# A fourth wide product in 14 of 22 feed-forward blocks, and a few reordered steps around the feed-forward part

## The chip, the cores and the metric

The kernel runs on one core of one Trainium2 chip. The metric is device time in microseconds of one execution; the time quoted for a kernel is the median of its runs. TensorE is called PE, VectorE DVE, ScalarE ACT, GpSimd POOL and SyncE SP, as in the profile.

## What is computed

One layer of a decoder on 512 tokens of width 1024 in float32: a mixer sublayer (stick-breaking attention beside a gated short convolution), cross-attention into 256 memory tokens, a SwiGLU feed-forward sublayer, a final norm. The change touches the feed-forward sublayer and the norm:

```python
def rms_norm(x, g):
    xf = x.astype(jnp.float32)
    var = jnp.mean(xf * xf, axis=-1, keepdims=True)
    return (xf * lax.rsqrt(var + EPS) * g.astype(jnp.float32)).astype(x.dtype)
...
        hf = rms_norm(x, norm_ffn[l])
        gate, up = jnp.split(hf @ w_ffn_in[l], 2, axis=-1)
        x = x + (jax.nn.silu(gate) * up) @ w_ffn_out[l]
    return rms_norm(x, norm_final)
```

The hidden width is 2816, which is 22 blocks of 128 gate columns and 128 up columns.

## The kernel before

**Two halves of a number.** PE multiplies in a shortened float32 format (F32R). Each operand is split: `hi` is its cast to F32R (on ACT), `lo` the rest (a subtraction on DVE: `rest_of`, L996). A product is then three multiplications: hi x hi, hi x lo, lo x hi.

**Seven products for eight.** The feed-forward input projection uses a scheme of the Strassen kind. The activations are cut in two along the tokens (256 each) and in two along the inner dimension; the weights likewise, and gate and up take the place of two output halves. `forms_of` makes seven activation forms (xf, xo, xc, a form of xd, xc, xd, xo, counted 0 to 6), and each weight block m has seven weight forms. So a block m is seven products (m, 0) to (m, 6), each over four inner slices k. They accumulate in three PSUM banks: z for the products 0, 3, 4, 5, v for 1, y for 2 and 6. `banks[m]` also holds the scratch tiles s ("sa"), t ("sb") and g ("fg").

**Narrow and wide products.** In `product` the products 0, 3, 4 and 5 are narrow: per slice three multiplications of 256 columns into the left half of z. The products 1, 2 and 6 are wide: their form lies with hi and lo side by side in one tile, so that one multiplication of 512 columns does hi x hi into the left half of the bank and hi x lo into the right (L906), and one of 256 columns adds lo x hi (L914). The halves of the bank are added when it is read (`joined_halves`, L932 and L933).

**Reading the results.** After the products 0, 3 and 4 ACT copies z to s or t (`reads`, L940). DVE joins v and y with those copies into g and t. `evict(m, 0..2)` then scales g by the norm's factor (L954), takes its silu on ACT (L956), and multiplies it by z and by t on DVE (L964): these are the activations for the output projection. `evict(m, 2)` runs one block later, at the product (m + 2, 0).

**Weights.** `ffn_load` brings a block's weights in with SP's DMA queue and adds two quarters with an accumulating DMA on POOL's queue. `sum_third` (L871) and `sum_last` (L875) make two more sums, on POOL for the blocks 0 to 2 and on DVE from 3 on. `pair_cast` and `third_cast` make the forms: a cast on ACT, and one or two products later the subtraction on DVE.

**Order.** The list `uses` gives the order of the products on PE: for a block m, (m,3), (m,2), (m,4), (m+1,0), (m+1,1), (m,5), (m,6). `todo` says which other step is issued after which entry of it (`at`, and `made` for a cast and its subtraction). PE, ACT and DVE execute in exactly that written order; each engine waits at an instruction whose operands are not there, and everything behind it waits too. PSUM gives four banks to z, two to v and two to y; the weight forms have four buffers each for hi and lo.

**The norm ahead of the feed-forward part.** The residual stream's squares are summed while the products already run, and `squares_mean` splits the sum in hi and lo (acch, accl). Two multiplications with a constant matrix give the mean (varb), then `rstd_of` makes the factor r0b: Ln and Exp on ACT, and a Newton step on DVE. Before the change these are issued after the entries 8 and 10 of `uses`.

**The end of the feed-forward part.** The casts and subtractions for the output projection's first blocks are interleaved with the last products (`begun`, `ended`; "w0" is a weight block, "x0" an activation).

## Time and profile before

| | us |
|---|---|
| median of 3 runs (lowest to highest) | 841.49 (841.46 to 842.75) |
| the profiled execution, its own time | 841.48 |
| its span in the trace | 839.8 |
| PE busy | 830.6 |
| DVE busy | 682.0 |
| ACT busy | 458.3 |
| POOL busy | 164.2 |
| feed-forward input products on PE, first to last | 502.6 to 723.8 |

A timeline row reads: start in us from the span's start, duration in us, engine, line, operation, what it writes from what it reads, shapes, count. A bracket at its end gives the time that the engine stood idle just before it and what ended this. Matmuls overlap: PE's pace is the distance of starts, and an end is modelled. In the feed-forward part the tile names say which product a row is: z<-xf is product 0, v<-xo 1, y<-xc 2, z<-xdh and z<-xdl 3 or 5, z<-xc 4, y<-xo 6.

### The profile page before, as it was taken

Reading aid. Unit: us, or ns where it says so; the run is one execution under the profiler, and the core shown is the slowest. Engines: PE = TensorE matmul, PEld = TensorE weight load, DVE = VectorE, ACT = ScalarE, POOL = GpSimd, SP = SyncE. Lnnn points to the kernel's source line nnn. Section 1 sums busy time; section 2 is a strip of 40 time slices with the busy share of each in tenths; the row PEclk is TensorE's granted clock in tenths of the full one; section 3 lists DMA queues with packets and bytes.
Section 4 is the critical chain, followed back from the end, with each engine's and each line's share of the span. In section 5 each row is a group of like instructions: output and inputs, shape, how many; then the busy total and the mean of one; then the engine's idle time right before and its main releaser. Section 6 shows DMA issues by size and latency. Waiting matters only on the chain.

```text
span 839.8 us, 12035 instructions
## 1 busy us (share of the span) xinstructions
PE 830.6 (99%) x4430; PEld 716.8 (85%) x4430; DVE 682.0 (81%) x1070; ACT 458.3 (55%) x778; POOL 164.2 (20%) x170
## 2 busy tenths in 40 slices
PE   9999999999999999999999999999999999999996
PEld 7888888888888888888888889999999999888885
DVE  7879899986756577586555689999999999999886
ACT  7567878674332355433444556644455545576654
POOL 0011131110666620173000032111111110000401
PEclk9999999999999999999999999999999999999999
DMA  8553454134687865556421326577767663465552
GB/s 302 153 167 101 121 115 112 61 121 167 235 314 274 314 230 199 188 229 235 151 75 51 101 65 161 152 180 198 200 170 204 179 181 96 165 216 197 178 184 101
DMA packets 51359, 143.70 MB, mean 171 GB/s; under 512 B 5762, under 2 KB 7042, under 8 KB 48483
## 3 DMA queue, kind: packets, MB, share of 16 engines
q1 hardware_dynamic: 41650, 107.89, 38.1%
q0 software_dynamic: 9360, 34.75, 15.6%
q8 instruction: 35, 0.57, 0.3%
q10 hardware_dynamic: 288, 0.28, 0.1%
q14 instruction: 26, 0.20, 0.1%
HBM read 125.20 MB, written 13.64 MB: 165 GB/s over the span
## 4 chain that ended last, share of the span: by engine, by line
PE 97%; DVE 1%; ACT 0%; issue 0%; DVEq 0%
PE z L911 14%; PE p L1216 12%; PE pr L156 8%; PE pr L158 8%; PE pr L157 8%; PE y L906 5%; PE r L157 3%; PE r L156 3%; PE r L158 3%; PE v L284 3%; PE v L906 2%; PE y L914 2%; PE km L662 2%; PE mq L158 2%; PE mq L156 2%; PE mq L157 2%
## 5 line engine op out<-in xcount | busy, mean ns | idle before, releaser
L151 ACT CAST wh<-wr 128x1024 fp32r<-128x1024 f32 x84 | 88.1, 1051 | 142.2 <-issue 75.3
L152 DVE TENSOR_TENSOR wl<-wr,wh 128x1024 fp32r<-128x1024 f32 x84 | 111.1, 1323 | 31.7 <-ACT wh L151 31.7
L156 PE MATMUL pr<-xgh,wh 128*128 128x512 f32 x288 | 112.8, 392 | 0.0
L157 PE MATMUL pr<-xgl,wh 128*128 128x512 f32 x288 | 112.3, 390 | 0.0
L158 PE MATMUL pr<-xgh,wl 128*128 128x512 f32 x288 | 112.2, 390 | 0.0
L607 POOL TENSOR_TENSOR pre<-pre 128x512 f32<-128x512 f32 x44 | 71.2, 1623 | 31.4 <-DMA pre<-in_w_ffn_out_dram 29.1
L859 POOL DMA_DIRECT2D ws<-in_w_ffn_in_dram x22 | 26.6, 1209 | 236.3 <-DVE c L704 53.9
L911 PE MATMUL z<-xdh,wf 128*128 128x256 f32 x352 | 70.0, 283 | 0.0
L158 PEld LDWEIGHTS pr<-xgh,wl 128*128 128x128 f32 x288 | 54.1, 188 | 11.6
L156 PEld LDWEIGHTS pr<-xgh,wh 128*128 128x128 f32 x288 | 54.1, 188 | 10.5
L157 PEld LDWEIGHTS pr<-xgl,wh 128*128 128x128 f32 x288 | 54.1, 188 | 10.5
L940 ACT COPY sa<-z 128x256 f32<-128x256 f32 x44 | 16.4, 373 | 78.9 <-PE z L911 76.7
L911 PEld LDWEIGHTS z<-xdh,wf 128*128 128x128 f32 x352 | 57.4, 190 | 0.1
L911 PE MATMUL z<-xdl,wf 128*128 128x256 f32 x176 | 49.7, 282 | 0.0
L996 DVE TENSOR_TENSOR wf<-wg,wf 128x1024 fp32r<-128x1024 f32 (+1 forms) x44 | 43.1, 979 | 1.6 <-ACT wf L884 0.2
L996 DVE TENSOR_TENSOR wl<-wr,wh 128x1024 fp32r<-128x1024 f32 x33 | 41.0, 1243 | 2.8 <-ACT wh L1063 2.8
L1063 ACT CAST wh<-wr 128x1024 fp32r<-128x1024 f32 x33 | 34.5, 1049 | 6.2 <-ACT f01h L992 2.6
L911 PE MATMUL z<-xf,wf 128*128 128x256 f32 x264 | 35.7, 283 | 0.0
L911 PE MATMUL z<-xc,wf 128*128 128x256 f32 x264 | 35.2, 283 | 0.2 <-ACT sa L940 0.2
L911 PEld LDWEIGHTS z<-xf,wf 128*128 128x128 f32 x264 | 33.4, 192 | 0.3 <-DVE wf L996 0.2
L911 PEld LDWEIGHTS z<-xc,wf 128*128 128x128 f32 x264 | 33.1, 190 | 0.5 <-ACT sa L940 0.4
L911 PEld LDWEIGHTS z<-xdl,wf 128*128 128x128 f32 x176 | 33.4, 190 | 0.0
(352 smaller groups left out, 2212.0 us busy)
## 6 DMA issues: line engine op xcount, KB each, us to landing
wr<-in_w_in_dram SPq DMA_DIRECT2D x36, 512.0 KB, 3.5
pre<-in_w_ffn_out_dram POOLq DMA_DIRECT2D x11, 1024.0 KB, 7.9
sums<-pre POOLq DMA_DIRECT2D x11, 1024.0 KB, 4.8
ws<-in_w_ffn_in_dram SPq DMA_DIRECT2D x22, 512.0 KB, 5.3
wg<-in_w_ffn_in_dram SPq DMA_DIRECT2D x22, 512.0 KB, 4.7
ws<-in_w_ffn_in_dram POOLq DMA_DIRECT2D x22, 512.0 KB, 5.8
wr<-sums SPq DMA_DIRECT2D x22, 512.0 KB, 3.9
wr<-in_w_ffn_out_dram SPq DMA_DIRECT2D x16, 512.0 KB, 4.0
```

Source lines behind the costliest of these rows:

```text
L151: after(nc.scalar.copy(h2, raw), lead[-1:])
L152: lows.append(nc.vector.tensor_tensor(out=l2, in0=raw, in1=f(h2), op=ALU.subtract))
L156: nc.tensor.matmul(ps, a[0], b[0], start=start, stop=False, **kw)
L157: nc.tensor.matmul(ps, a[0], b[1], start=False, stop=False, **kw)
L158: nc.tensor.matmul(ps, a[1], b[0], start=False, stop=stop, **kw)
L607: nc.gpsimd.tensor_tensor(out=t[:, a, :], in0=t[:, a, :], in1=t[:, b, :], op=ALU.add)
L859: nc.gpsimd.dma_start(s13, a[:, 0:4:3, :], accum_op=ALU.add)
L906: nc.tensor.matmul(ps, hi, both[0], start=i < 3 and k == 0, stop=False, skip_group_check=True)
L911: nc.tensor.matmul(ps[:, :HS], a, b, start=i < 3 and k == 0 and j == 0, stop=k == KP - 1 and j == 2, skip_group_check=True)
L996: nc.vector.tensor_tensor(out=lo, in0=src, in1=f(hi), op=ALU.subtract)
L1063: nc.scalar.copy(hi, raw)
L1216: nc.tensor.matmul(res[i][s2], a[:, ts], b, start=j == 0 and n == 0, stop=n == 2 and j == (BEHIND - 1 if (i, s2) == (5, 1) else NJ - 1))
```

## The change

1. **The sixth product is wide in 14 blocks.** `forms_of` lays the forms 3 and 5 with hi and lo side by side, as it did the others: two casts and two subtractions of 256 columns in place of one each of 512. In the blocks 5 to 18 (`WIDE`) product 5 takes the wide branch, into the whole of z. ACT then copies z's right half to s, and `evict(m, 2)` adds it to z's left half on DVE before the multiplication. The order of the products stays.
2. **The norm's factor.** `rstd_of` folds two DVE operations into one. The sum's split is issued after entry 6 in place of 8, the mean after 8 in place of 10, its DVE part after 9.
3. **Two sums change their engine.** `sum_third(2)` and `sum_last(2)` run on DVE in place of POOL. One cast is issued an entry earlier.
4. **The last two blocks.** `sum_last(21)` is issued after (20,4) in place of (21,1); the cast of its result one entry earlier; the cast "x0" one entry later.

DVE around the mean, before (acch and accl are the split sum; ra and r0b the factor; wf the weight forms):

```order
L996 TENSOR_TENSOR wf_4867<-ws_4757,wf_4866 128x1024
L932 TENSOR_TENSOR sb_4786<-y_4804,sb_4786 128x256
L933 TENSOR_TENSOR sb_4786<-y_4804,sb_4786 128x256
L996 TENSOR_TENSOR wf_4915<-wg_4840,wf_4914 128x1024
L196 CAST acch_4929<-acc_4354 128x512
L197 TENSOR_TENSOR accl_4930<-acc_4354,acch_4929 128x512
L932 TENSOR_TENSOR fg_4797<-y_4804,sa_4785 128x256
L933 TENSOR_TENSOR fg_4797<-y_4804,fg_4797 128x256
L996 TENSOR_TENSOR wf_4946<-a_4761,wf_4945 128x1024
L126 TENSOR_SCALAR rv_4963<-varb_4960 128x512
L128 TENSOR_TENSOR ra_4965<-ry_4964 128x512
L129 SCALAR_TENSOR_TENSOR ra_4965<-ra_4965,rv_4963 128x512
```

and now:

```order
L1006 TENSOR_TENSOR wf_4869<-ws_4759,wf_4868 128x1024
L201 CAST acch_4906<-acc_4348 128x512
L202 TENSOR_TENSOR accl_4907<-acc_4348,acch_4906 128x512
L1006 TENSOR_TENSOR wf_4904<-wg_4842,wf_4903 128x1024
L936 TENSOR_TENSOR sb_4788<-y_4806,sb_4788 128x256
L937 TENSOR_TENSOR sb_4788<-y_4806,sb_4788 128x256
L129 SCALAR_TENSOR_TENSOR ra_4939<-ry_4938 128x512
L131 SCALAR_TENSOR_TENSOR ra_4939<-varb_4935,ra_4939 128x512
L133 SCALAR_TENSOR_TENSOR r0b_4940<-ra_4939,ry_4938 128x512
L936 TENSOR_TENSOR fg_4799<-y_4806,sa_4787 128x256
L937 TENSOR_TENSOR fg_4799<-y_4806,fg_4799 128x256
L1006 TENSOR_TENSOR wf_4956<-a_4763,wf_4955 128x1024
```

The split sum moved ahead of a subtraction and of the pair that reads y; the factor is made ahead of the next pair, with three operations in place of four; the sum wg (L874) follows the last row shown.

ACT at the end of the feed-forward part (the copies of z, the last block's casts, "w0" as wh, "x0" as f01h), before:

```order
L940 COPY sa_7209<-z_7208 128x256
L884 CAST wf_7226<-ws_7015 128x1024
L884 CAST wf_7255<-a_7095 128x1024
L1063 CAST wh_7260<-wr_7258 128x1024
L992 CAST f01h_7263<-a_5063 128x512
L940 COPY sa_7209<-z_7208 128x256
L1000 CAST fh_7282<-a_5064 128x256
```

and now:

```order
L946 COPY sa_7182<-z_7181 128x256
L887 CAST wf_7199<-ws_6989 128x1024
L887 CAST wf_7214<-a_7066 128x1024
L1073 CAST wh_7233<-wr_7231 128x1024
L946 COPY sa_7182<-z_7181 128x256
L1002 CAST f01h_7250<-a_5063 128x512
L1010 CAST fh_7253<-a_5064 128x256
```

The second copy of z moved ahead of f01h; the DVE sum that the cast of a waits for is issued four DVE operations earlier.

ACT in one of the 14 blocks, now (the row of L944 is new, the others stand as before):

```order
L946 COPY sa_5467<-z_5466 128x256
L887 CAST wf_5487<-ws_5269 128x1024
L944 COPY sa_5352<-z_5351 128x256
L887 CAST wf_5518<-wg_5386 128x1024
L946 COPY sa_5467<-z_5466 128x256
```

The new copy of z's right half stands between two casts, and waits there for product 5 of the older block.

```diff
-    def rstd_of(var, n, s, tables=()):
+    def rstd_of(var, n, s, tables=(), later=False):
...
-        v, y, a = new("rv"), new("ry"), new("ra")
+        y, a = new("ry"), new("ra")
         r = cpool.tile([P, n], F32, tag=s, name=nm(s))
         after(nc.scalar.activation(y, var, AF.Ln, bias=eps_t), tables)
-        nc.vector.tensor_scalar(out=v, in0=var, scalar1=EPS, scalar2=None, op0=ALU.add)
         exps.append(nc.scalar.activation(y, y, AF.Exp, scale=-0.5))
-        nc.vector.tensor_tensor(out=a, in0=y, in1=y, op=ALU.mult)
-        nc.vector.scalar_tensor_tensor(out=a, in0=a, scalar=-0.5, in1=v, op0=ALU.mult,
-                                       op1=ALU.mult)
-        nc.vector.scalar_tensor_tensor(out=r, in0=a, scalar=1.5, in1=y, op0=ALU.add, op1=ALU.mult)
-        return r
+
+        def refined():
+            nc.vector.scalar_tensor_tensor(out=a, in0=y, scalar=-0.5, in1=y, op0=ALU.mult,
+                                           op1=ALU.mult)
+            nc.vector.scalar_tensor_tensor(out=a, in0=var, scalar=EPS, in1=a, op0=ALU.add,
+                                           op1=ALU.mult)
+            nc.vector.scalar_tensor_tensor(out=r, in0=a, scalar=1.5, in1=y, op0=ALU.add,
+                                           op1=ALU.mult)
+            return r
+
+        return refined if later else refined()
...
         second, fourth = beside(n1, "xc"), beside(t3, "xc")
-        dh, dl = split(d, "xd")
+        third, fifth = beside(n2, "xd"), beside(t4, "xd")
         last = beside(b22, "xo")
-        return [(u[:, a], u[:, b]), first, second, (dh[:, a], dl[:, a]), fourth[:2],
-                (dh[:, b], dl[:, b]), last]
+        return [(u[:, a], u[:, b]), first, second, third[:2], fourth[:2], fifth, last]
...
-            if both:
+            if both and (i != 5 or m in WIDE):
...
+    WIDE = range(5, NF - 3)
...
-        if i in (0, 3, 4):
+        if i == 5 and m in WIDE:
+            nc.scalar.copy(s[:, :HS], b["z"][:, HS:])
+        elif i in (0, 3, 4):
...
-            for half, u in enumerate((b["z"][:, :HS], b["t"][:, HS:])):
+            first = b["z"][:, :HS]
+            if m in WIDE:
+                first = b["s"][:, :HS]
+                nc.vector.tensor_tensor(out=first, in0=b["z"][:, :HS], in1=first, op=ALU.add)
+            for half, u in enumerate((first, b["t"][:, HS:])):
...
-    made(7, pair_cast, 2, 0)
+    made(6, pair_cast, 2, 0)
     made(9, pair_cast, 1, 2)
-    at(9, lambda: sum_third(2, nc.gpsimd))
+    at(10, lambda: sum_third(2))
...
-        at(q[1], lambda m=m: sum_last(m + 1)) if m > 1 else at(11, lambda: sum_last(2, nc.gpsimd))
+        at(q[1] if m < NF - 2 else p[4], lambda m=m: sum_last(m + 1))
...
     n = uses.index((NF - 2, 5))
-    made(n, pair_cast, NF - 1, 2)
-    at(n, lambda: begun("w0", out_cast, *w01(0))(), begun("x0", cast_first, 0))
-    at(n + 1, ended("w0"), ended("x0"), begun("x2", half_form, 2, 0, 0))
-    at(n + 2, ended("x2"), lambda: n2_of(halves(acts[0][1])[0], 0), begun("x1", cast_first, 1))
+    made(n - 1, pair_cast, NF - 1, 2)
+    at(n, lambda: begun("w0", out_cast, *w01(0))())
+    at(n + 1, ended("w0"), begun("x0", cast_first, 0), begun("x2", half_form, 2, 0, 0))
+    at(n + 2, ended("x0"), ended("x2"), lambda: n2_of(halves(acts[0][1])[0], 0), begun("x1", cast_first, 1))
...
-            if n == 8:
+            if n == 6:
                 mean2 = mean2()
-            elif n == 10:
-                r2b[0] = mean2[0]("r0b", bank=mmtile)
+            elif n == 8:
+                mean2 = mean2[0]("r0b", bank=mmtile, later=True)
+            elif n == 9:
+                r2b[0] = mean2()
                 turn_r2()
```

More of the change, by code (lines that the diff above doesn't have):

```diff
@@ L203, in mean, with along @@
             return vp
-        def along(s, tables=(), bank=otile):
-            vp = mean(bank)
-            return rstd_of(vp, n * P, s, tables)
+        def along(s, tables=(), bank=otile, later=False):
+            return rstd_of(mean(bank), n * P, s, tables, later)
         def turned(s, tables=(), bank=otile):
```

## The prediction

> **What bounds the kernel now.** I read the page first, then the feed-forward stretch by windows, then the instruction timeline around every place where TensorE (PE) left its rhythm. The page's engine row:
>
> ```profile
> PE 830.6 (99%) x4430; PEld 716.8 (85%) x4430; DVE 682.0 (81%) x1070; ACT 458.3 (55%) x778; POOL 164.2 (20%) x170
> ```
>
> A window inside the feed-forward blocks (us of the window; busy us and instruction groups of PE, weight loads, DVE, ACT, POOL; clock; DMA):
>
> ```profile
> 564.00:700.00 136.00, 136.00 (x987) 128.84 (x987) 127.48 (x213) 67.84 (x109) 16.86 (x14) 1.00 0.70 185
> ```
>
> PE is the bound: it is busy all 136.00 us of that window at full clock. VectorE (DVE) has 127.48 of them. So time can change in two ways only: PE's own work gets shorter, or PE's few waits go or come. The next fence is the timeline of one steady block (start, duration, engine, line, operation).
>
> ```profile
> 602.66 1.09 PE L906 MATMUL v<-xo,wf 128*128 128x512 f32 x4
> ...
> 604.06 0.28 PE L911 MATMUL z<-xdh,wf 128*128 128x256 f32 x1
> ...
> 604.14 1.05 ACT L884 CAST wf<-wg 128x1024 fp32r<-128x1024 f32 x1
> ...
> 604.33 0.42 DVE L932 TENSOR_TENSOR fg<-v,sa 128x256 f32<-128x256 f32 x1
> ...
> 604.79 0.42 DVE L933 TENSOR_TENSOR fg<-v,fg 128x256 f32<-128x256 f32 x1
> ...
> 605.38 0.28 PE L911 MATMUL z<-xdh,wf 128*128 128x256 f32 x1
> ...
> 605.50 1.09 PE L906 MATMUL y<-xo,wf 128*128 128x512 f32 x4
> ...
> 607.89 1.22 DVE L996 TENSOR_TENSOR wf<-wg,wf 128x1024 fp32r<-128x1024 f32 x1
> ...
> 611.16 1.60 PE L911 MATMUL z<-xf,wf 128*128 128x256 f32 x12
> ...
> 612.60 1.09 PE L906 MATMUL v<-xo,wf 128*128 128x512 f32 x4
> ```
>
> A product in the wide form (four 512-column and four 256-column multiplications) lasts from 602.66 to 604.06, 1.40 us; one in the narrow form (twelve of 256 columns) from 604.06 to 605.50, 1.44 us, as from 611.16 to 612.60. From v to v a block takes 9.94 us, four narrow and three wide products without a gap. So a 256-column step costs 0.12 us and a 512-column one (1.40 - 4 x 0.12) / 4 = 0.23.
>
> **Term 1: the fourth wide product.** It removes twelve narrow multiplications and adds four wide and four narrow: 1.44 - 1.40 = 0.04 us, or 0.03 where rounding goes the other way. In 14 blocks 0.4 to 0.6; I take 0.45. Below nothing it cannot go on PE, since three products of each block already run in this form.
>
> The Trainium skill, TensorE: Matmul & The Clock Gate, section Back-to-back issue gap, gives N/2.4 + 2.5 ns for a single multiplication's gap; by that the narrow form is an estimated 1.31 us and the wide 1.30, and the term would be some 0.15 us. Here the trace disagrees with the level (1.44 and 1.40) and I use the trace.
>
> The price is one more ACT copy and one more DVE addition of 128x256 per block. The copy must wait for the sixth product's end, 605.38 + 0.28 = 605.66, and stands ahead of the cast of wg that ran at 604.14. With 0.37 for the copy (the row of such a copy, 0.36, is in the last fence) the cast ends at 605.66 + 0.37 + 1.05 = 607.1; DVE's subtraction of it began at 607.89, so 0.8 us are left and the copy costs nothing. If that cover were gone, DVE would wait for ACT once per block.
>
> The addition is a DVE operation that the next one depends on: 604.33 to 604.79, 0.46 us. Whether DVE has room is read where it ran without pause, from one sum of the weights to the next:
>
> ```profile
> 531.59 0.69 DVE L871 TENSOR_TENSOR wg<-ws,wg 128x512 f32<-128x512 f32 x1
> ...
> 540.73 0.69 DVE L871 TENSOR_TENSOR wg<-ws,wg 128x512 f32<-128x512 f32 x1
> ...
> 550.32 0.69 DVE L871 TENSOR_TENSOR wg<-ws,wg 128x512 f32<-128x512 f32 x1
> ```
>
> An odd and an even block take 9.14 + 9.59 = 18.73 us of DVE; PE needs 2 x 9.94 = 19.88, then 19.82. With 0.92 added DVE needs 19.65. That fits by 0.17 us in two blocks: thin, but the lateness does not grow. The nearest cover behind it is the weight form that DVE finishes at 607.89 + 1.22 = 609.11 and PE first reads at 611.16, 2.05 us. I cost the addition at nothing; above 0.54 us each it would begin to eat that cover.
>
> **Term 2: PE's waits at the start of the feed-forward part.** These are PE's rows there:
>
> ```profile
> 515.38 0.28 PE L911 MATMUL z<-xdh,wf 128*128 128x256 f32 x1
> ...
> 518.21 0.40 PE L202 MATMUL varb<-acch,mean_r 128*128 128x512 f32 x1
> ...
> 518.85 0.50 PE L202 MATMUL varb<-accl,mean_r 128*128 128x512 f32 x1 [0.24 <-DVE accl L197]
> ...
> 524.77 0.28 PE L911 MATMUL z<-xdh,wf 128*128 128x256 f32 x1
> ...
> 525.43 1.21 PE L906 MATMUL y<-xo,wf 128*128 128x512 f32 x4 [0.38 <-DVE sb L933]
> ...
> 531.22 1.84 PE L911 MATMUL z<-xf,wf 128*128 128x256 f32 x12
> ...
> 532.89 1.09 PE L906 MATMUL v<-xo,wf 128*128 128x512 f32 x4
> ...
> 534.61 0.28 PE L911 MATMUL z<-xdl,wf 128*128 128x256 f32 x1
> ```
>
> From 518.21 to 524.77 PE should run two mean multiplications (0.23 each), then xc, xf, v and eleven steps of xd: 0.46 + 1.44 + 1.44 + 1.40 + 1.32 = 6.06; it took 6.56, so 0.50 went at the mean. From 524.77 to 525.43 it took 0.66 for a step of 0.12: 0.54. From 525.43 to 531.22 two wide and two narrow products, 5.68, took 5.79: 0.11. Then 531.22 to 532.89, 1.67 for 1.44: 0.23; and 532.89 to 534.61, 1.72 for 1.40 + 0.12: 0.20. Together 1.58 us. Why DVE was late:
>
> ```profile
> 512.08 1.22 DVE L996 TENSOR_TENSOR wf<-ws,wf 128x1024 fp32r<-128x1024 f32 x1
> ...
> 516.67 0.42 DVE L196 CAST acch<-acc 128x512 fp32r<-128x512 f32 x1
> ...
> 516.85 1.39 POOL L871 TENSOR_TENSOR wg<-ws,wg 128x512 f32<-128x512 f32 x1 [9.60 <-DVE wf L996]
> ...
> 517.13 1.67 DVE L197 TENSOR_TENSOR accl<-acc,acch 128x512 fp32r<-128x512 f32 x1
> ...
> 519.09 1.75 POOL L875 TENSOR_TENSOR a<-wg 128x512 f32<-128x512 f32 x1
> ...
> 519.39 0.69 ACT L125 ACTIVATE ry<-varb,eps_t 128x512 f32<-128x512 f32 x1 [2.95 <-PE varb L202]
> ...
> 519.50 2.43 DVE L996 TENSOR_TENSOR wf<-a,wf 128x1024 fp32r<-128x1024 f32 x1
> ...
> 523.16 0.69 DVE L129 SCALAR_TENSOR_TENSOR ra<-ra,rv 128x512 f32<-128x512 f32 x1
> ...
> 524.95 0.42 DVE L933 TENSOR_TENSOR sb<-y,sb 128x256 f32<-128x256 f32 x1
> ...
> 530.34 1.22 DVE L996 TENSOR_TENSOR wf<-wg,wf 128x1024 fp32r<-128x1024 f32 x1
> ```
>
> While POOL's two sums ran, accl took 1.67 us (0.69 for its size elsewhere) and the subtraction at 519.50 took 2.43 (1.22 elsewhere): 2.2 us lost on DVE. The Trainium skill, SBUF — State Buffer, section Who interferes with whom, says that a DVE instruction with two SBUF inputs contends with a GpSimd instruction that reads SBUF. The trace agrees, with those two rows.
>
> The change puts both sums on DVE (2 x 0.61, start to start), takes one 512-wide operation out of rstd (0.60), and splits a cast's subtraction in two (0.08): DVE pays 0.7 and gets back 2.2. It also moves the mean ahead by one product. By row durations: the subtraction of 512.08 ends at 513.30, acch and accl end at 514.5; PE reaches the mean at 515.38, so it no longer waits and runs it in 0.46. Wf<-wg 1.22 and the sb pair 0.87 bring DVE to 516.6. Ln and Exp, 0.7 each, follow the mean until about 517.4; three operations of 0.72 end r0b at 519.6. Then the fg pair 0.8, wf<-a 1.22, the sum 0.61 and the sb pair 0.87: 523.0. PE gets to the product that waited for sb at 515.38 + 0.46 + 4 x 1.44 + 2 x 1.40 = 524.4, with 1.4 us to spare. Going on in the same way (0.6 + 0.8 + 0.6 + 0.6 + 1.13 + 0.8 + 1.1, then 1.22) DVE ends the form that PE waited for at 531.22 at about 529.9; PE needs its low half at 524.4 + 5.68 + 0.24 = 530.3. Here only 0.4 is left. The mean's 0.50 and the 0.65 around 525.43 I count whole, of the last two (0.43) I count 0.3: 1.45. Bounds 0.5 and 1.6. The wait that would be next is that same form, at the third block's first product.
>
> **Term 3: the wait at the end of the feed-forward part.**
>
> ```profile
> 714.47 0.68 DVE L875 TENSOR_TENSOR a<-wg 128x512 f32<-128x512 f32 x1
> ...
> 715.23 1.05 ACT L884 CAST wf<-a 128x1024 fp32r<-128x1024 f32 x1 [1.65 <-issue]
> ...
> 716.18 1.04 ACT L1063 CAST wh<-wr 128x1024 fp32r<-128x1024 f32 x1
> ...
> 717.19 0.63 PE L914 MATMUL y<-xc,wf 128*128 128x256 f32 x4
> ...
> 717.66 0.36 ACT L940 COPY sa<-z 128x256 f32<-128x256 f32 x1
> ...
> 718.07 1.69 PE L911 MATMUL z<-xc,wf 128*128 128x256 f32 x12 [0.24 <-ACT sa L940]
> ...
> 719.60 0.63 PE L906 MATMUL y<-xo,wf 128*128 128x512 f32 x2
> ```
>
> PE took 0.88 us from 717.19 instead of 4 x 0.12, and 1.53 instead of 1.44 for the next product: 0.50 us, waiting for a copy that stood behind three ACT casts. The change issues the DVE sum four operations earlier, the first cast one product earlier and the activation's cast behind the copy. Four such operations are some 1.6 us, and ACT was idle for 1.65 us before 715.23; so it has both weight casts done by 715.23 - 1.6 + 1.05 + 1.04 = 715.7. The copied product ends only with the start of the next one at 717.19 - 0.93 = 716.3, and the copy then follows at once, a whole product ahead of its reader. I take 0.50, bounds 0 and 0.5. The activation's cast then starts no later than now, and its reader, the output projection, starts only after the three products from 719.60 on.
>
> **Sum.** The profiled execution: 841.48 us for a span of 839.8, 1.7 around it; it lies 0.01 under the median of 841.49. 841.48 - 0.45 - 1.45 - 0.5 = 839.08; **839.1 us**, 0.28% faster.
>
> **Rivals.**
> (a) The start's waits move instead of going. DVE carries all the sums now and the margin at the third block is 0.4 us. If only the mean's 0.5 comes, 841.48 - 0.45 - 0.5 - 0.5 = 840.0: no change that shows.
> (b) The tail gives nothing, because ACT waits for another cast: 841.48 - 0.45 - 1.45 = 839.6.
> (c) The issue-gap rule decides for the fourth wide product: 0.15 in place of 0.45, 839.4. Against it stand the three wide products in each block.
> (d) DVE becomes the bound in the 14 blocks, on the other side. The place is the addition ahead of the activations' multiplication, or the cast behind the copy. If it takes 0.92 us start to start instead of 0.46, each block is 0.92 - 0.54 = 0.38 late, 5.3 in 14 blocks; 2.05 are covered, and PE waits 3.3: 842.3. It turns slower than before from (2.4 + 2.05) / 14 + 0.54 = 0.86 us each. For it: the 0.17 us of room. Against it: POOL's sums, which doubled DVE's rows above, do not run in those blocks.
>
> **Chances.** Forecast 0.60 (838.7 to 839.6), (a) 0.20, (b) 0.08, (c) 0.04, (d) 0.08, some of that within no change. A change under 0.2% (1.7 us) can't be told from none here. So faster (under 839.8) 0.70: the forecast nearly whole, (b), (c) and a little of (a); same 0.24; slower 0.06. The range 838.5 to 840.7 leaves out most of (d) and nothing below except unseen gains.
>
> **What would show it.** Right: xd in those blocks as four 512- and four 256-column rows lasting 1.40 us; accl at 0.69 with no bracket behind the mean; no bracket at y<-xo about 524; sa<-z right behind its product near 714; DVE near 9.8 busy of 9.9 in the 14 blocks. Wrong: brackets naming DVE wf or ACT wf on PE rows after 560, or a block longer than 9.94.

## The result, and the profile after

The changed kernel takes 839.61 us (median of 8 runs, 838.75 to 839.88); the kernel before, beside it, 841.62 (8 runs, 841.39 to 842.75). The medians lie 2.0 us apart. The ratio is 0.9972, with a 95% interval of 0.9963 to 0.9981: faster by 0.28%, which is 2.4 us of 841.62. A second, later measurement gave 839.33 us and 0.9971 (0.9959 to 0.9983).

The profiled execution took 838.75 us for a span of 837.0, against 841.48 and 839.8 before. Its engine row, and the row that gives the chain of waits by engine:

```profile
PE 828.8 (99%) x4374; PEld 714.1 (85%) x4374; DVE 684.6 (82%) x1086; ACT 463.9 (55%) x796; POOL 161.2 (19%) x168
...
PE 99%; DVE 0%; ACT 0%; DVEq 0%; issue 0%
```

PE is still the bound. It issues 56 multiplications fewer (14 blocks, eight in place of twelve), DVE and ACT some more operations. Windows inside the feed-forward blocks (us; busy us and instruction groups of PE, weight loads, DVE, ACT, POOL; clock; DMA):

```profile
560.00:690.00 130.00, 130.00 (x896) 120.86 (x895) 125.87 (x217) 70.49 (x119) 16.86 (x14) 1.00 0.70 186
580.00:680.00 100.00, 100.00 (x690) 92.97 (x689) 96.98 (x167) 54.07 (x91) 12.04 (x10) 1.00 0.70 185
```

PE is busy for all of both windows, and DVE shows 3% idle. The profile's list of PE's waits by the engine it waited for, over the whole program, is now one row, the wait at PE's warm-up:

```profile
PE warm L248 <- DVE neg L92: 1.4, 1, 1.4
```

The three rows that stood beside it before (0.4 us at y behind DVE's sb, 0.2 at z behind ACT's sa, 0.2 at the mean behind accl) are gone.

From the first product's first multiplication of the feed-forward part to the first one of the output projection PE took 221.25 us before (502.58 to 723.83) and takes 218.78 now (502.38 to 721.16). By the starts of the products v the 2.47 us come from three places: 1.59 where PE waited at the start (from the last slice of block 0's v, at 507.20, to block 4's v it was 14.86 + 10.83 + 10.13 = 35.82 and is 14.35 + 9.94 + 9.94 = 34.23), 0.38 in the 14 blocks (9.94 to 9.913 each), and 0.50 at the end (11.83 to 11.33). Of the span's 2.8 us, 0.2 lie ahead of the feed-forward part and 0.14 behind PE's last multiplication, which the change doesn't touch.

PE at the start of the part, after:

```profile
515.18 0.40 PE L207 MATMUL varb<-acch,mean_r 128*128 128x512 f32 x1
515.41 0.39 PE L207 MATMUL varb<-accl,mean_r 128*128 128x512 f32 x1
515.64 1.59 PE L914 MATMUL z<-xd,wf 128*128 128x256 f32 x12
...
524.17 1.09 PE L909 MATMUL y<-xo,wf 128*128 128x512 f32 x4
...
529.84 1.60 PE L914 MATMUL z<-xf,wf 128*128 128x256 f32 x12
531.28 1.09 PE L909 MATMUL v<-xo,wf 128*128 128x512 f32 x4
...
532.68 1.59 PE L914 MATMUL z<-xd,wf 128*128 128x256 f32 x12
```

No row has a bracket, and from 515.18 every start is the sum of what stands ahead of it. DVE there:

```profile
511.94 1.22 DVE L1006 TENSOR_TENSOR wf<-ws,wf 128x1024 fp32r<-128x1024 f32 x1
513.07 0.42 DVE L201 CAST acch<-acc 128x512 fp32r<-128x512 f32 x1
513.52 0.69 DVE L202 TENSOR_TENSOR accl<-acc,acch 128x512 fp32r<-128x512 f32 x1
514.13 1.22 DVE L1006 TENSOR_TENSOR wf<-wg,wf 128x1024 fp32r<-128x1024 f32 x1
...
517.22 0.69 DVE L129 SCALAR_TENSOR_TENSOR ra<-ry 128x512 f32<-128x512 f32 x1 [1.08 <-ACT ry L126]
...
522.26 0.42 DVE L937 TENSOR_TENSOR sb<-y,sb 128x256 f32<-128x256 f32 x1
...
528.26 1.22 DVE L1006 TENSOR_TENSOR wf<-wg,wf 128x1024 fp32r<-128x1024 f32 x1
```

accl lasts 0.69 us in place of 1.67; the sb that PE waited for ends at 522.68, 1.5 us ahead of its reader at 524.17; the form of the third block (block 3) ends at 529.48, and PE needs its low half some 0.24 after 529.84.

A block with the fourth wide product:

```profile
600.75 1.09 PE L909 MATMUL v<-xo,wf 128*128 128x512 f32 x4
...
602.15 1.09 PE L909 MATMUL z<-xd,wf 128*128 128x512 f32 x4
603.08 0.64 PE L917 MATMUL z<-xd,wf 128*128 128x256 f32 x4
603.56 1.09 PE L909 MATMUL y<-xo,wf 128*128 128x512 f32 x4
603.76 0.37 ACT L944 COPY sa<-z 128x256 f32<-128x256 f32 x1 [1.43 <-PE z L917]
604.03 1.06 ACT L887 CAST wf<-wg 128x1024 fp32r<-128x1024 f32 x1
...
610.66 1.09 PE L909 MATMUL v<-xo,wf 128*128 128x512 f32 x4
```

The product lasts from 602.15 to 603.56, 1.41 us; the block 9.91. The new copy follows its product, and the cast behind it ends at 605.09. The end of the part:

```profile
711.30 1.05 ACT L887 CAST wf<-a 128x1024 fp32r<-128x1024 f32 x1
...
712.25 1.05 ACT L1073 CAST wh<-wr 128x1024 fp32r<-128x1024 f32 x1
...
714.28 0.37 ACT L946 COPY sa<-z 128x256 f32<-128x256 f32 x1 [0.98 <-PE z L914]
714.54 0.63 ACT L1002 CAST f01h<-a 128x512 fp32r<-128x512 f32 x1
...
715.02 0.63 PE L917 MATMUL y<-xc,wf 128*128 128x256 f32 x4
...
715.49 1.60 PE L914 MATMUL z<-xc,wf 128*128 128x256 f32 x12
...
716.92 1.09 PE L909 MATMUL y<-xo,wf 128*128 128x512 f32 x4
```

ACT is idle for 0.98 us before the copy and takes it as soon as its product is over. PE's 0.47 and 1.43 us for the two products are those of the steady blocks.

### The profile page after: what moved, and what is told of

It reads as the page before. It is cut to its first block, busy times and chain, and to the rows that moved or that the text cites. A ratio compares the mean times of both kernels' runs of the same rounds, so it can differ in the third digit from the quotient of the medians.

```text
span 837.0 us, 11962 instructions
## 1 busy us (share of the span) xinstructions
PE 828.8 (99%) x4374; PEld 714.1 (85%) x4374; DVE 684.6 (82%) x1086; ACT 463.9 (55%) x796; POOL 161.2 (19%) x168
## 4 chain that ended last, share of the span: by engine, by line
PE 99%; DVE 0%; ACT 0%; DVEq 0%; issue 0%
PE z L914 13%; PE p L1228 12%; PE pr L161 8%; PE pr L162 8%; PE pr L163 8%; PE y L909 5%; PE r L162 3%; PE r L163 3%; PE r L161 3%; PE v L288 3%; PE y L917 2%; PE v L909 2%; PE km L666 2%; PE mq L163 2%; PE mq L161 2%; PE mq L162 2%
## 5 line engine op out<-in xcount | busy, mean ns | idle before, releaser
L914 PE MATMUL z<-xd,wf 128*128 128x256 f32 x360 | 47.5, 282 | 0.0
L914 PEld LDWEIGHTS z<-xd,wf 128*128 128x128 f32 x360 | 45.0, 190 | 0.1
L368 DVE TENSOR_TENSOR g<-pr,r0b 128x512 f32<-128x512 f32 x16 | 11.0, 687 | 23.5 <-PE pr L163 23.5
L417 POOL TENSOR_SCALAR_AFFINE_SELECT e<-e 128x128 f32<-128x128 f32 (+1 forms) x24 | 10.7, 447 | 86.6 <-DVE e L470 86.6
```

Of the source, the lines that this page charges most:

```text
L914: nc.tensor.matmul(ps[:, :HS], a, b, start=i < 3 and k == 0 and j == 0, stop=k == KP - 1 and j == 2, skip_group_check=True)
```

## The experiments

Where the time came from is plain from the trace; why it came is not, since the change makes several edits in each place. The experiments take them apart. Each was timed beside the kernel before (medians 841.83 to 841.85 us; ratios are to it). Since times of one kernel spread by a microsecond, sizes below that are read from each kernel's trace. "Lost at the end" is the time from the last v to the output projection over 11.33 us. "Lost at the start" is what is left of the feed-forward part's length over 219.16 us, its length without a wide sixth product and without a wait (over 218.78 us with the wide product in 14 blocks); by the starts of v it comes out the same within 0.02.

### The start: which edit took the wait away

**POOL's two sums alone** (the prediction's reason for DVE's lateness). The kernel before, with

```diff
-    at(9, lambda: sum_third(2, nc.gpsimd))
+    at(10, lambda: sum_third(2))
...
-        at(q[1], lambda m=m: sum_last(m + 1)) if m > 1 else at(11, lambda: sum_last(2, nc.gpsimd))
+        at(q[1], lambda m=m: sum_last(m + 1))
```

> The kernel before with one part of the change alone: the two sums of block 2 run on DVE in place of POOL (wg<-ws,wg after entry 10, a<-wg after (2,1)). My theory: POOL's sums slow DVE (accl 1.67 us, one subtraction 2.43 us), and DVE's lateness makes PE wait. Then accl takes 0.69 us and ends at about 517.8, before PE's mean at 518.2; sb ends near 524.0, before PE needs it; of the 1.58 us of PE's losses between 502 and 535 at least 1.2 go: PE from the first product of the feed-forward part to its last 221.25 - 1.2 = about 220.0 us, time 840.3. Rival: the place of the mean and of the factor's operations decides, and the two sums only cost DVE 1.2 us more; then the losses stay near 1.6 us and the time near 841.5.

Measured: 841.46 us, ratio 0.9997 (0.9987 to 1.0006), and 1.29 us lost at the start, against 1.59 before. That is nearer to the rival than to the theory. accl is at 0.69 us and the wait at the mean is gone, as it should be. But the time turned up elsewhere on DVE:

```profile
514.86 0.43 DVE L932 TENSOR_TENSOR sb<-y,sb 128x256 f32<-128x256 f32 x1 [1.28 <-ACT sb L940]
...
517.41 0.69 DVE L197 TENSOR_TENSOR accl<-acc,acch 128x512 fp32r<-128x512 f32 x1
518.69 0.42 DVE L932 TENSOR_TENSOR fg<-y,sa 128x256 f32<-128x256 f32 x1 [0.59 <-PE y L914]
...
530.31 1.22 DVE L996 TENSOR_TENSOR wf<-wg,wf 128x1024 fp32r<-128x1024 f32 x1
```

DVE still stands for 1.28 us before the first sb pair, waiting for ACT's copy of a product, as it did in the kernel before:

```profile
514.58 0.43 DVE L932 TENSOR_TENSOR sb<-y,sb 128x256 f32<-128x256 f32 x1 [1.29 <-ACT sb L940]
```

And behind the shorter accl it now waits 0.59 for the next product. Of the 2.19 us that POOL's sums had cost (1.67 - 0.69 and 2.43 - 1.22), 0.59 go to that wait and 1.2 to the two sums, now DVE's own: some 0.4 remain. The form ends at 531.53, and PE waits for it:

```profile
PE z L911 <- DVE wf L996: 0.6, 1, 0.6
```

**The mean and its factor alone**, with the sums left on POOL: from the kernel before, the three-operation `rstd_of` with `later`, and

```diff
-            if n == 8:
+            if n == 6:
                 mean2 = mean2()
-            elif n == 10:
-                r2b[0] = mean2[0]("r0b", bank=mmtile)
+            elif n == 8:
+                mean2 = mean2[0]("r0b", bank=mmtile, later=True)
+            elif n == 9:
+                r2b[0] = mean2()
                 turn_r2()
```

> The kernel before with another part alone: the norm's factor (three DVE operations in place of four, the split sum, the mean and the factor issued two entries earlier); the sums stay on POOL. My theory: POOL's sums now lie beside other DVE operations and slow those, so DVE stays 1 us or more later than in the whole change: the mean's 0.5 us goes, and the waits at the third block (0.43 us) stay or grow. PE's loss between 502 and 535 is 0.4 to 1.0 us, time 840.5 to 841.1. Rival (the place of the mean decides): no wait is left, loss under 0.2 us, time 840.0.

Measured: 840.52 us, ratio 0.9984 (0.9975 to 0.9994), 0.09 us lost at the start, as the rival had it. So this part alone takes 1.50 of the 1.59, while POOL's sums still stretch what DVE does beside them:

```profile
514.39 0.42 DVE L936 TENSOR_TENSOR sb<-y,sb 128x256 f32<-128x256 f32 x1 [0.22 <-ACT sb L944]
...
516.66 1.29 POOL L875 TENSOR_TENSOR wg<-ws,wg 128x512 f32<-128x512 f32 x1 [9.63 <-DVE wf L1000]
...
517.24 1.26 DVE L129 SCALAR_TENSOR_TENSOR ra<-ry 128x512 f32<-128x512 f32 x1 [0.67 <-ACT ry L126]
...
518.53 0.69 DVE L131 SCALAR_TENSOR_TENSOR ra<-varb,ra 128x512 f32<-128x512 f32 x1
518.67 1.74 POOL L879 TENSOR_TENSOR a<-wg 128x512 f32<-128x512 f32 x1
...
519.26 1.71 DVE L133 SCALAR_TENSOR_TENSOR r0b<-ra,ry 128x512 f32<-128x512 f32 x1
...
528.65 1.22 DVE L1000 TENSOR_TENSOR wf<-wg,wf 128x1024 fp32r<-128x1024 f32 x1
```

Two factor operations take 1.26 and 1.71 us where 0.69 is their length: 1.6 us go to POOL, in place of the 2.2 before. The operation between them reads the mean (varb) from PSUM and keeps its 0.69, although POOL's second sum runs beside it. DVE's wait before sb is 0.22 us in place of 1.29, since the split sum now runs in it, but a wait of 0.67 for Exp has come in front of the factor.

**The saved operation alone**, at the old place: the kernel before, with the three-operation `rstd_of` and nothing else.

```diff
-        nc.vector.tensor_scalar(out=v, in0=var, scalar1=EPS, scalar2=None, op0=ALU.add)
...
-        nc.vector.tensor_tensor(out=a, in0=y, in1=y, op=ALU.mult)
-        nc.vector.scalar_tensor_tensor(out=a, in0=a, scalar=-0.5, in1=v, op0=ALU.mult,
-                                       op1=ALU.mult)
+            nc.vector.scalar_tensor_tensor(out=a, in0=y, scalar=-0.5, in1=y, op0=ALU.mult,
+                                           op1=ALU.mult)
+            nc.vector.scalar_tensor_tensor(out=a, in0=var, scalar=EPS, in1=a, op0=ALU.add,
+                                           op1=ALU.mult)
```

> The kernel before with the factor's three DVE operations in place of four alone, at the old place; the mean and the sums as before. It tells apart what of the moved mean's part decides. DVE saves 0.6 us behind the mean. My theory (the place of the split sum decides, which fills DVE's wait of 1.3 us for the copy of z): the mean's 0.5 us and the waits at the third block (0.4 us or more) stay, only the wait for sb (0.65 us) goes: PE's loss between 502 and 535 is 0.8 to 1.2 us. Rival (the saved operation decides): under 0.4 us.

Measured: 841.41 us, ratio 0.9993 (0.9984 to 1.0003), 1.28 lost, a little over the range. The operation's 0.60 is saved, but the subtraction beside POOL's second sum took 2.69 us in this execution, 0.26 more than in that of before.

**The earlier place alone**, with four operations and the sums on POOL:

```diff
+        def refined():
+            nc.vector.tensor_scalar(out=v, in0=var, scalar1=EPS, scalar2=None, op0=ALU.add)
+            nc.vector.tensor_tensor(out=a, in0=y, in1=y, op=ALU.mult)
...
-            if n == 8:
+            if n == 6:
                 mean2 = mean2()
-            elif n == 10:
-                r2b[0] = mean2[0]("r0b", bank=mmtile)
+            elif n == 8:
+                mean2 = mean2[0]("r0b", bank=mmtile, later=True)
+            elif n == 9:
+                r2b[0] = mean2()
```

> The kernel before with the split sum, the mean and the factor two entries earlier, but with four DVE operations; the sums stay on POOL. With three operations this part alone left under 0.2 us of PE's loss, and DVE ended the form for the third block 0.2 us ahead of its reader. My theory: 0.6 us more on DVE come back there in part: PE's loss 0.3 to 0.7 us, so the place brings 0.9 us or more of 1.58 and the operation the rest. Rival: the place alone brings all, loss under 0.2 us.

Measured: 841.24 us, ratio 0.9989 (0.9980 to 0.9999), 0.87 lost: a little over the range, and PE's first stop is earlier than expected, at a product of block 1. One factor operation took 2.50 us beside POOL's second sum:

```profile
519.62 2.50 DVE L131 SCALAR_TENSOR_TENSOR ra<-ra,rv 128x512 f32<-128x512 f32 x1
...
524.82 0.50 PE L914 MATMUL z<-xdh,wf 128*128 128x256 f32 x2 [0.59 <-DVE wf L999]
```

Here this operation reads two tiles in SBUF (ra and rv); in the run with three operations the one in its place read varb in PSUM and took 0.69. The fourth operation, rv, cost nothing by itself: it ran while DVE waited for Exp, and the first ra starts 14.84 us after the part's first multiplication, against 14.85 with three operations. By these rows, what the shorter factor adds to the earlier place, 0.78 us at the third block's form, is POOL's stretch (2.39 against 1.59 us) and not the operation's own 0.60.

**The whole change with the sums back on POOL:**

```diff
-    at(10, lambda: sum_third(2))
+    at(9, lambda: sum_third(2, nc.gpsimd))
...
-        at(q[1] if m < NF - 2 else p[4], lambda m=m: sum_last(m + 1))
+        at(q[1] if m < NF - 2 else p[4], lambda m=m: sum_last(m + 1)) if m > 1 else at(11, lambda: sum_last(2, nc.gpsimd))
```

> The changed kernel with the two sums of block 2 back on POOL (L871 and L875 as before). After the run with the mean moved alone, in which PE lost almost nothing although POOL's sums still stretched DVE's rows: my new theory says that the place of the mean decides and the sums are spare: PE's loss between 502 and 535 stays under 0.2 us, time within 0.2 us of the changed kernel. My first theory (POOL's sums make DVE late) says that 0.4 us or more come back at the third block.

Measured: 839.77 us, ratio 0.9974 (0.9965 to 0.9984); the feed-forward part takes 218.78 us, as with the sums on DVE, and nothing is lost. In the whole change the move of the sums is worth nothing.

**What decides, in one number.** All these kernels have one event in common: the end of DVE's subtraction for the third block's first product (the row at 530.34 in the kernel before). Counted from the feed-forward part's first multiplication, it says what PE loses. The last three columns take apart the time from the start of the subtraction at 512.08 (9.5 to 9.6 us after the first multiplication in every row) to this event: how much longer DVE's rows were than elsewhere, how long DVE stood (the brackets of its rows), and the rest, which is its own work.

| kernel | first multiplication | form ends | after | lost at the start | stretched | stood | own work |
|---|---|---|---|---|---|---|---|
| before | 502.58 | 531.56 | 28.98 | 1.59 | 2.19 | 1.29 | 16.0 |
| before, sums on DVE | 502.86 | 531.53 | 28.67 | 1.29 | 0 | 1.87 | 17.3 |
| before, three operations | 503.42 | 532.06 | 28.64 | 1.28 | 2.45 | 1.28 | 15.4 |
| before, earlier place | 503.47 | 531.73 | 28.26 | 0.87 | 2.39 | 0.21 | 16.2 |
| before, place and three operations | 502.39 | 529.87 | 27.48 | 0.09 | 1.59 | 0.89 | 15.5 |
| changed kernel | 502.38 | 529.48 | 27.10 | 0 | 0 | 1.08 | 16.5 |
| changed, sums on POOL | 503.54 | 530.18 | 26.64 | 0 | 0.75 | 1.07 | 15.3 |

In every row the loss is what lies above 27.39 us, within 0.03 (28.98 - 27.39 = 1.59, 28.26 - 27.39 = 0.87, 27.48 - 27.39 = 0.09). So PE's five stops of the old trace were one thing, DVE's lateness, paid in instalments; the form's end marks it, though PE need not stop at this form (with the earlier place it stopped at an earlier form, the row in brackets above). An edit is worth what it moves that event, down to 27.4 and not further. The changed kernel has 0.3 us to spare, with the sums left on POOL 0.75.

No single column decides. The earlier place alone removes most of DVE's standing, the sums' move alone removes the stretch but pays with own work and more standing, and in the changed kernel DVE stands for 1.08 us again, now for Exp. With the sums on POOL the changed kernel has a stretch of 0.75 us (one factor operation at 1.44), less than the 1.2 that the sums cost DVE; in the run with place and three operations it was still 1.59. Between these two lies, beside the wide product and its forms, the cast issued an entry earlier: the subtraction behind it, which POOL's first sum waits for, comes earlier, and this sum starts 13.1 us after the first multiplication in place of 14.3. No run has this cast alone, so what it is worth is not shown.

### The end: which half of the edit

Two edits, each alone in the kernel before: the activation's cast one product later, and the sum with its cast earlier.

```diff
-    at(n, lambda: begun("w0", out_cast, *w01(0))(), begun("x0", cast_first, 0))
-    at(n + 1, ended("w0"), ended("x0"), begun("x2", half_form, 2, 0, 0))
-    at(n + 2, ended("x2"), lambda: n2_of(halves(acts[0][1])[0], 0), begun("x1", cast_first, 1))
+    at(n, lambda: begun("w0", out_cast, *w01(0))())
+    at(n + 1, ended("w0"), begun("x0", cast_first, 0), begun("x2", half_form, 2, 0, 0))
+    at(n + 2, ended("x0"), ended("x2"), lambda: n2_of(halves(acts[0][1])[0], 0), begun("x1", cast_first, 1))
```

> The kernel before with the cast x0 alone issued one entry later at the end of the feed-forward part. The copy of z then stands behind two ACT casts in place of three, starts at about 717.2 and ends at 717.5, PE is due at 717.67. My theory: the whole 0.50 us of this wait goes, time 841.0, though the DVE sum is where it was. Rival: the late DVE sum decides, and 0.2 us or more of the wait stay.

```diff
-        at(q[1], lambda m=m: sum_last(m + 1)) if m > 1 else at(11, lambda: sum_last(2, nc.gpsimd))
+        at(q[1] if m < NF - 2 else p[4], lambda m=m: sum_last(m + 1)) if m > 1 else at(11, lambda: sum_last(2, nc.gpsimd))
...
-    made(n, pair_cast, NF - 1, 2)
+    made(n - 1, pair_cast, NF - 1, 2)
```

> The kernel before with the other half alone: the DVE sum of the last block after (20,4) and the cast of its result one entry earlier, x0 where it was. The three casts then start some 1.6 us earlier, x0 ends at about 716.3, and the copy follows its product. My theory: the whole 0.50 us goes too, so that either half of this part is enough; time 841.0. Rival: the weight block w0 or the sum comes later than thought, the copy stays late, and 0.2 us or more remain.

Measured: nothing lost at the end with either, 0.50 without. One half would have done. With the activation's cast moved, the copy stands ahead of f01h, though still behind two casts:

```profile
717.45 1.05 ACT L1063 CAST wh<-wr 128x1024 fp32r<-128x1024 f32 x1
718.40 0.36 ACT L940 COPY sa<-z 128x256 f32<-128x256 f32 x1
718.66 0.62 ACT L992 CAST f01h<-a 128x512 fp32r<-128x512 f32 x1
```

With the sum moved, f01h stays ahead, and all of ACT's work is done early enough:

```profile
715.20 0.62 ACT L992 CAST f01h<-a 128x512 fp32r<-128x512 f32 x1
...
716.29 0.37 ACT L940 COPY sa<-z 128x256 f32<-128x256 f32 x1 [0.47 <-PE z L911]
```

By the times neither shows: 841.33 us, 0.9995 (0.9986 to 1.0005), and 841.73, 0.9997 (0.9988 to 1.0007). Half a microsecond is 0.06%, below what these measurements tell. Nothing in the two edits reaches the start, and the start lost 2.12 us in the one trace and 1.45 in the other (the form ends 29.53 and 28.85 us after the first multiplication, 2.14 and 1.46 above 27.39): POOL's second sum stretched the same subtraction to 2.98 and to 2.31 us.

### The blocks: the fourth wide product and DVE's room

**Without the wide product:** the changed kernel with

```diff
-    WIDE = range(5, NF - 3)
+    WIDE = range(0)
```

> The changed kernel with no wide sixth product at all (no copy of z's right half, no addition; the forms still lie side by side). My theory: the fourth wide product is worth what PE's steps say, 14 x (1.435 - 1.405) = 0.4 us, and DVE's addition costs nothing on the path: every block lasts 9.94 us again, PE's feed-forward part 218.78 + 0.4 = 219.2 us, time 0.4 us above the changed kernel's. Rival: the addition and the copy eat the gain somewhere, then the time without them is the same or lower.

Measured: 839.89 us, ratio 0.9977 (0.9967 to 0.9986); the blocks take 9.94 us and the feed-forward part 219.16, which is 0.38 more than with it.

**One more dependent addition in each of the 14 blocks** of the changed kernel, on DVE, as the rival for the other side had it (the line adds zero times the value to the value, which stays as it is):

```diff
                 nc.vector.tensor_tensor(out=first, in0=b["z"][:, :HS], in1=first, op=ALU.add)
+                nc.vector.scalar_tensor_tensor(out=first, in0=first, scalar=0.0, in1=first,
+                                               op0=ALU.mult, op1=ALU.add)
```

> The changed kernel with one more DVE operation of 128x256 in each of the 14 blocks, which adds nothing to the result (0 x first + first) and stands between the addition and its reader. By my rows DVE then needs 18.73 + 4 x 0.46 = 20.57 us for two blocks and PE 19.82: 0.75 late in two blocks, 5.2 in 14; some 2 are covered, PE waits about 3.2 us: time about 842.8, the blocks near 10.2 us once the cover is gone. Rival: DVE has more room than its rows say, no PE wait, time 839.6.

Measured: 843.9 us, ratio 1.0022 (1.0012 to 1.0031), slower than before. The feed-forward part takes 222.74 us, 3.96 more and not the 3.2 expected. Six of the blocks still take 9.91 us, and then PE follows DVE, here by the starts of v and the waits of two blocks:

```profile
641.08 1.09 PE L909 MATMUL v<-xo,wf 128*128 128x512 f32 x4
...
648.16 0.74 PE L917 MATMUL y<-xc,wf 128*128 128x256 f32 x4 [0.34 <-DVE wf L1008]
...
651.61 1.09 PE L909 MATMUL v<-xo,wf 128*128 128x512 f32 x4
...
661.66 0.63 PE L909 MATMUL v<-xo,wf 128*128 128x512 f32 x2
```

Two blocks take 661.66 - 641.08 = 20.58 us. The prediction's count of DVE's work gives 19.65 + 2 x 0.46 = 20.57. So DVE's need of 19.65 in two blocks of the changed kernel, which that kernel's own trace can't show since DVE keeps PE's pace there, is right, and the room is 0.17 of 19.82. The cover was taken too large: 14 blocks are 14 x 0.38 = 5.3 us late and PE waited 4.0, so 1.3 were covered and not 2.05. The row in brackets says why: PE waits for the low half of another product's form (xc), not for that of the product I had named (xf).

**The wide product in 21 blocks, and in all 22:**

```diff
-    WIDE = range(5, NF - 3)
+    WIDE = range(1, NF)
```

> The changed kernel with the wide sixth product in the blocks 1 to 21 in place of 5 to 18. By PE's steps 7 x 0.03 = 0.2 us less: 839.4. My theory: in the blocks 1 to 4 DVE still works off its lateness of the start (it has 0.28 us of room in a block, and 0.46 go), but it was 0.6 us ahead of its first reader there and loses no more than 0.2 per block, so PE waits 0 to 0.6 us; at the end the output projection's first subtractions move by 0.5 us or less and are read more than 1 us later. Time 839.2 to 840.0. Rival: the early or the last blocks are past DVE's room, PE waits 1 us or more, time above 840.5.

```diff
-    WIDE = range(5, NF - 3)
+    WIDE = range(NF)
```

> The changed kernel with the wide sixth product in all 22 blocks. With 21 blocks PE lost nothing in the feed-forward part and it lasted 218.59 us; block 0 adds 0.03: 218.56 us. My theory: no PE wait in the feed-forward part, time 0.2 us under the changed kernel's, which timing can hardly tell. Rival: block 0's copy and addition fall into DVE's and ACT's busiest stretch, behind the mean, and 0.3 us or more come back at the third block.

Measured: in 21 blocks the part takes 218.59 us, 0.19 less than in 14, without a wait of PE; in 22 it takes 218.86, with blocks of 10.03 and 10.07 at the start. The one addition more lies ahead of the third block's form and ends it 27.63 us after the first multiplication, 0.24 over the 27.39 of the table. So the rival came there. The times, 839.68 us (0.9973, 0.9963 to 0.9983) and 839.72 (0.9975, 0.9965 to 0.9985), can't tell either from the changed kernel, which was run once more:

> The changed kernel again, for a second trace beside the next one. The feed-forward part on PE lasts 218.8 us as before; the time differs from the first trace only by what PE loses in the first 12 us (0.1 us in the first trace, 0.9 to 5 us in others): 838.7 to 840.5.

Measured: 839.33 us, its feed-forward part 218.78.

## Why the prediction was right, and where it was not

The forecast was 839.1 us, with a range of 838.5 to 840.7; 839.61 came. By the time alone this could also be rival (b), priced at 839.6; the traces tell them apart.

**The bound** held: PE is busy in the whole of the blocks' windows, before and after, and the time changed only where its work got shorter or its waits went. One sign did not come as written: DVE "near 9.8 busy of 9.9" in the 14 blocks is 96.98 of 100 us, 9.6 of 9.91. DVE's addition starts at 601.20 and lasts 0.41 us, the multiplication that depends on it starts at 601.65; such gaps count as idle although they are no room.

**Term 1** (0.45 forecast): 0.38, shown by the trace and by taking the wide product out. It is 0.027 us in each block, so the 0.04 of single rows was rounding. By the issue gap of the Trainium skill (TensorE: Matmul & The Clock Gate, section Back-to-back issue gap) it would be an estimated 0.14, which the prediction rounded to 0.15; the measurement lies nearer to the rows. The copy cost nothing, for the reason given: forecast to end the cast behind it 4.4 us after v (607.1 against 602.66), it ended 4.3 after (605.09 against 600.75). The addition cost nothing, and the thin room of 0.17 us in two blocks was confirmed by adding a second one. The cover named behind it was wrong in place and size (1.3 us, another product's form); with one addition it isn't used.

**Term 2** (1.45 forecast): 1.59. The size and the event times were right: sb forecast to end at 523.0, seen at 522.68; the third block's form at 529.9, seen at 529.48. The margin of 0.4 at that form is 0.6 by the rows (529.48 against 529.84 + 0.24) and 0.3 by the table; where the other 0.3 goes was not followed. It held, so the 0.13 that I left out came too, and rival (a) did not.

What does not hold is the use made of "why DVE was late". That POOL's two sums stretch DVE is right: 2.19 us before, the largest of the delays in the table, and none in the changed kernel. The Trainium skill, SBUF — State Buffer, section Who interferes with whom, has the rule for it. But the prediction read from this that the sums' move brings the time back, and the move is neither enough nor needed: alone it returned 0.3 of the 1.59 us, since DVE then pays 1.3 us more work and stands 0.6 us more, and undone in the whole change it costs PE nothing. The earlier place of the split sum, the mean and the factor, with the shorter factor, brings 1.50 without it; these three moved together, and no run has the split sum's place alone. They start Ln and Exp 3.5 us earlier (515.84 against 519.39).

The sum came out right because it followed the order of the whole change, event by event. Its balance, DVE pays 0.7 and gets back 2.2, is 0.5 and 2.2 in the table. But such a balance of the whole says nothing of a single edit, and it left out that DVE also stood in the kernel before: 1.29 us ahead of the first sb pair, waiting for ACT.

**Term 3** (0.50 forecast): 0.50. The casts are done, the copy follows its product, a product ahead of its reader. Not foreseen: each half of the edit is enough.

**Rivals.** (b) fell with term 3, (c) with term 1. (d) was priced at 842.3 us and the extra addition, which makes its condition true, gave 843.9: the break-even was right, the cover was not.

**The half microsecond above the forecast** isn't in the part that changed, as far as two traces show. The forecast was made for the profiled execution, and this came out at 838.75, the fastest of the eight and 0.33 below the forecast of 839.08: 0.14 more than forecast at the start of the part, 0.2 ahead of it and 0.14 behind it, less the 0.07 of term 1 and another 0.07 around the span. The other runs of the same kernel are up to 1.1 us longer. In the second trace of the changed kernel the feed-forward part is equally long (218.78), and starts at 502.90 in place of 502.38: the 0.5 us come before it.

## What to carry to other kernels

When an engine is late, take its time apart into work, stretch and standing before naming a cause: a faster operation in front of a wait only lengthens the wait, an operation moved into idle time can cost nothing, and a delay can be removed in more than one way, so that what one edit is worth depends on the others. Before pricing several stalls in a row, look for the one event that causes them all (here the end of one weight form); edits are then worth how far they move it, down to a threshold, and their gains don't add. A margin as thin as 0.17 us in 19.8 held here because each term was taken start to start from rows; the cover behind it has to be read for every reader, not for the nearest one.

## What the runs showed that was not expected

**The first 12 us differ from one execution to the next.** The start of DVE's cast of the first loaded weights, in the changed kernel's profile:

```profile
4.32 0.43 DVE L257 CAST wvh<-wk 128x512 fp32r<-128x512 f32 x1 [1.95 <-DMA wk<-in_w_value_dram]
```

and in that of the kernel with 21 wide blocks, whose program is the same up to there:

```profile
5.27 0.43 DVE L257 CAST wvh<-wk 128x512 fp32r<-128x512 f32 x1 [2.89 <-DMA wk<-in_w_value_dram]
...
5.84 2.05 PE L288 MATMUL v<-wvh,xgh 128*128 128x512 f32 x4 [0.69 <-DVE wvh L257]
```

The load came 0.95 us later, PE stopped at its first products, and by the feed-forward part this execution was 3.2 us behind (505.60 against 502.38); it took 841.88 us while the kernel's median is 839.68. The other 2.3 us went in the first twelve multiplications: they took 5.09 us (5.84 to 10.93) in place of 2.79 (4.93 to 7.72), at a granted clock of 1.00 in both traces. Why they were slow is open. Over the traces of all these kernels the feed-forward part starts between 502.38 and 505.60. This spread is larger than what most of these edits are worth, which is why their sizes are read from the trace.

**The stretch lasts until POOL's sum is done.** The same subtraction of 128x1024, 1.22 us alone, took 2.31, 2.43, 2.69 and 2.98 us beside the same sum of POOL in four executions in which the code around it is the same or almost so. In all four it ended 1.08 or 1.09 us after POOL's sum, a little less than its own length: in the kernel before at 521.93, with POOL's sum ending at 520.84. The stretched rows of 128x512 in these traces ended 0.54 to 0.57 us after the sum beside them. So the size is set by how much of POOL's sum is left when DVE's operation comes, and this differs between executions. Rows that read one of their operands from PSUM kept their length (0.42 us at 519.16 in the kernel before, while POOL's second sum ran).
